# Attention kernel: sums of a row's halves and high parts of the values on ScalarE, grouped-query outputs read by ScalarE and added by GpSimd

## The chip, the cores and the metric

The kernel runs on one core of a Trainium2 chip. The metric is the device time of one execution in microseconds (us). Engines are named as the profile names them: PE is TensorE, DVE is VectorE, ACT is ScalarE, POOL is GpSimd, and SP is the engine whose queue issues the DMA transfers. Each engine carries out its own instructions in the order in which they stand in its queue; between engines, an instruction waits on semaphores for what it needs.

## What is computed

One layer of a hybrid block over 2048 latent tokens and 256 context tokens of width 1024: a modulated RMS norm, one input projection, three mixers (pooling, differential attention, grouped-query attention), a gate on each, and two output projections. The change touches the two attentions, which read 2304 keys (context and latent):

```python
def _diff_core(q, k, v, lam):              # 4 heads, two score maps each
    s = jnp.einsum('bqhcd,bkhcd->bhcqk', q, k).astype(jnp.float32) * (DIFF_HEAD_DIM ** -0.5)
    p = jax.nn.softmax(s, axis=-1)
    a = (p[:, :, 0] - lam * p[:, :, 1]).astype(v.dtype)
    return jnp.einsum('bhqk,bkhe->bqhe', a, v)

def _gqa_core(q, k, v):                    # 8 query heads, 2 key/value heads
    s = jnp.einsum('bqgrd,bkgd->bgrqk', q, k).astype(jnp.float32) * (GQA_HEAD_DIM ** -0.5)
    p = jax.nn.softmax(s, axis=-1).astype(v.dtype)
    return jnp.einsum('bgrqk,bkgd->bqgrd', p, v)
```

All values are 32-bit floats. The kernel feeds TensorE with 16-bit pairs, a high part and the remainder as a low part, and adds up the products.

## The kernel before

There are three stages. The first projects queries, keys and values and writes them to memory; it lasts until about 560 us. The second, from 560 to about 2330 us, is the attention, mixed with the gate projection (line 179), which is independent of it and fills PE. The third (from about 2404 us) is the branch and output projections. The change lies in the second stage alone.

**Rows.** The second stage goes through 256 *rows*. A row is 128 queries of one head against all 2304 keys. The rows come in fours: d0 and d1 (the two score maps of a differential head), then g0 and g1 (two query tiles of a grouped-query head). `score_row` does one row:

- PE writes the scores into two PSUM tiles, `sa` (1024 keys) and `sb` (1280 keys), of which there is one buffer each (L812).
- DVE takes the negated maximum of each half (L815, L816) and combines the two (L817), all into the small tile `nm` of four columns.
- ACT does the exponentials of both halves (L820, L821) into `pt`, each with the sum of its half accumulated into `nm` (columns 2 and 3). Only when these are done may PE write the next row's `sa` and `sb`.

**What follows a row.** `inverse_sum` on DVE adds the two half sums and scales them (L825), and takes the reciprocal (L827). For the differential rows it runs at the head of the next row's place; at d1 it is followed by the ratio of the two maps (L866). For grouped-query rows it stands at the head of the place two rows later, inside `high`. `combine` (DVE, L870) merges d0 and d1. `high` (ACT, L874 or L898) writes the 16-bit high part of the probabilities, `low` (DVE, L879 or L903) the remainder; both are transposed by DMA (L849), and the products with the values (`diff_av` L917, `gqa_av` L941 and L947) are done on PE four rows later.

**The order** of all engines is written out by hand: the order in which the Python code emits instructions is the order in each engine's queue. The loop over `i` emits, for each row: what tables `ahead` and `split_later` hold for this place, then the row, then `todo` and `after`, then PE's filling (products with the values, then gate units). On DVE a *slot*, from one L817 to the next, therefore reads: L817 of this row; splits of values, if any; `combine` or `low`; readings of PE's filling; then the small instructions at the head of the next place; the next row's L815 and L816. On ACT it reads: both exponentials; readings of PE's filling; `high` of an earlier row; the next exponentials.

**Readings of PE's filling.** A finished gate unit is read by ACT (`gt`, L188); in 48 units, those of the SiLU paths, DVE multiplies it (L191). A finished grouped-query product has its two halves in partitions 0 to 63 and 64 to 127 of PSUM: ACT copies the upper one (`sh`, L954), and DVE scales the lower one and adds (L955), into `ot`.

**Values.** When a head begins, `load_values` fetches its values in six parts of three key tiles. DVE writes the high part (L798) and the low part (L800) of each into `vt`. Two parts are split in one slot, so each load takes three slots. A differential load has parts of 128x384, a grouped-query load parts of 128x192.

## Time and profile before

| | |
|---|---|
| median of 3 runs | 2884.64 us (2880.09 to 2886.94) |
| the profiled execution | 2881.96 us, of which its span is 2880.2 us |
| busy, share of the span | PE 95%, DVE 77%, ACT 56%, POOL 24% |
| mean granted TensorE clock | 0.987 of full speed |

The span runs from the first to the last instruction; 1.8 us lie outside it. Busy time of PE is modelled and includes the pipelined end of every product, so a stretch in which PE is busy throughout is one without gaps, not one at the peak. The share of an engine over the whole span mixes stages with different limits; the second stage is read slot by slot below.

### The profile page before, as it was taken

The page shows a single profiled execution, that of the slowest core. Times are in us where ns is not written, and L with a number is a line of the kernel's source. Part 1 is how long each engine was busy: PE and PEld are TensorE (multiplying, and loading weights), DVE is VectorE, ACT ScalarE, POOL GpSimd, SP SyncE. Part 2 cuts the span into 40 slices and gives each one's busy share as a digit, 9 for nine tenths or more (in the row PEclk, how much of TensorE's full clock was granted, in tenths as well). Part 3 has the DMA queues.
Part 4 walks back from the last instruction along what each step waited for, and adds up shares of the span by engine and source line. Part 5 has one row for each costly group of instructions (what it writes and reads, how often), then busy time and mean ns, then how long its engine had stood idle before and what let it go on. Part 6 is the DMA issues. An engine that isn't in the chain of part 4 may idle for free. (4 is left out here: it accounts for less than half of the span.)

```text
span 2880.2 us, 41085 instructions
## 1 busy us (share of the span) xinstructions
PE 2739.0 (95%) x15031; PEld 1592.2 (55%) x15031; DVE 2216.1 (77%) x2829; ACT 1624.4 (56%) x2168; POOL 700.0 (24%) x699
## 2 busy tenths in 40 slices
PE   7999999999999989999989999999999988999999
PEld 2544435645555445545545555555555546787787
DVE  4446657499888898889989999899998956766753
ACT  3844432267766666767756777676777742322221
POOL 1035645411111102110202111112111114443421
PEclk8999999999999999999999999999999998999999
DMA  7345552488988888888898999998998876767664
GB/s 258 110 122 160 132 161 64 112 172 175 187 166 170 179 184 168 171 178 179 170 196 190 185 188 185 177 206 178 186 187 173 177 164 230 248 225 258 208 244 147
DMA packets 1134266, 516.46 MB, mean 179 GB/s; under 512 B 985040, under 2 KB 1038704, under 8 KB 1134064
## 3 DMA queue, kind: packets, MB, share of 16 engines
q1 hardware_dynamic: 1134064, 513.84, 75.9%
q8 instruction: 118, 1.93, 0.3%
q14 instruction: 84, 0.69, 0.1%
HBM read 208.24 MB, written 78.97 MB: 100 GB/s over the span
## 5 line engine op out<-in xcount | busy, mean ns | idle before, releaser
L179 PE MATMUL gate<-hT,gws 128*128 128x512 f16 x3840 | 871.6, 380 | 0.5 <-ACT gt L185 0.5
L179 PEld LDWEIGHTS <-gws 128*128 128x128 f16 x3840 | 368.6, 98 | 432.0 <-issue 32.9
L820 ACT ACTIVATE pt<-sa,nm,escale 128x1024 f32<-128x1024 f32 x256 | 308.4, 1205 | 427.0 <-DVE nm L817 387.6
L812 PEld LDWEIGHTS <-qt 128*128 128x128 f16 x2560 | 249.8, 98 | 380.5 <-issue 100.9
L532 PE MATMUL qkv<-wt,hT 128*128 128x512 f16 (+1 forms) x1920 | 391.6, 358 | 0.0
L816 DVE TENSOR_REDUCE nm<-sb 128x1 f32<-128x1280 f32 x256 | 378.9, 1480 | 2.1 <-PE sb L812 2.1
L821 ACT ACTIVATE pt<-sb,nm,escale 128x1280 f32<-128x1280 f32 x256 | 360.5, 1408 | 0.0
L815 DVE TENSOR_REDUCE nm<-sa 128x1 f32<-128x1024 f32 x256 | 310.8, 1214 | 49.6 <-PE sa L812 41.1
L903 DVE SCALAR_TENSOR_TENSOR lo<-pt,nm,hi 128x2304 f16<-128x2304 f32 x128 | 337.8, 2639 | 8.6 <-ACT hi L898 4.7
L812 PE MATMUL sb<-kt,qt 128*128 128x512 f16 (+1 forms) x1536 | 320.5, 345 | 24.9 <-ACT pt L821 24.7
L898 ACT ACTIVATE hi<-pt,nm 128x2304 f16<-128x2304 f32 x128 | 283.3, 2213 | 92.0 <-issue 46.7
L812 PE MATMUL sa<-kt,qt 128*128 128x512 f16 x1024 | 262.6, 379 | 35.9 <-ACT pt L820 35.0
L532 PEld LDWEIGHTS <-hT 128*128 128x128 f16 x1920 | 187.1, 98 | 173.7 <-issue 9.1
L1193 PE MATMUL br<-bt,wt 128*128 128x512 f32 x1152 | 268.6, 394 | 1.6 <-DVE wt L1048 1.6
L1193 PEld LDWEIGHTS br<-bt,wt 128*128 128x128 f32 x1152 | 217.9, 189 | 51.0 <-DVE wt L1048 2.7
L927 POOL TENSOR_TENSOR o<-ot 128x256 f32<-128x256 f32 x32 | 19.8, 620 | 837.3 <-ACT ot L923 706.9
L163 POOL TENSOR_SCALAR gws<-gw 128x512 f16<-128x512 f32 x74 | 69.3, 936 | 605.9 <-PE gate L179 602.2
L917 PE MATMUL av<-th,vt 128*128 128x256 f16 x1728 | 198.9, 273 | 0.0
L1225 PE MATMUL out<-y,wt 128*128 128x512 f32 x768 | 186.2, 401 | 11.6 <-DVE wt L1048 4.9
L917 PEld LDWEIGHTS <-vt 128*128 128x128 f16 x1728 | 169.1, 98 | 19.8
L1225 PEld LDWEIGHTS out<-y,wt 128*128 128x128 f32 x768 | 145.4, 190 | 51.5 <-DVE wt L1048 8.1
L870 DVE SCALAR_TENSOR_TENSOR pt<-pt,nm 128x2304 f32<-128x2304 f32 x64 | 168.9, 2640 | 0.0
(209 smaller groups left out, 3222.9 us busy)
## 6 DMA issues: line engine op xcount, KB each, us to landing
tD<-gt SPq DMA_DIRECT2D x96, 256.0 KB
wr<-in_w_br SPq DMA_DIRECT2D x32, 768.0 KB
ld<-tD SPq DMA_DIRECT2D x96, 256.0 KB
scan<-in_w_gate SPq DMA_DIRECT2D x40, 512.0 KB
gw<-in_w_gate SPq DMA_DIRECT2D x80, 256.0 KB
qt<-qD SPq DMA_DIRECT2D x256, 64.0 KB
wr<-in_w_out SPq DMA_DIRECT2D x32, 512.0 KB
sgD<-gt SPq DMA_DIRECT2D x48, 256.0 KB
```

The costliest lines, as they stand in the source:

```text
L179: nc.tensor.matmul(ps, lhsT=w[:, b, k, :], rhs=hT[k][:, a, c * CH:(c + 1) * CH], start=(n == 0), stop=(n == 3 * KT - 1))
L532: nc.tensor.matmul(ps[:, :width], lhsT=tokens_of(t, k, a), rhs=wt[k][:, b, :width], start=(n == 0), stop=(n == 3 * KT - 1))
L812: nc.tensor.matmul(dst, lhsT=qt[:, s, o * P:(o + 1) * P], rhs=kt[:, k0:k1], start=(s == 0), stop=(s == 1))
L815: nc.vector.tensor_reduce(out=nm[:, 0:1], in_=sa, axis=AX.X, op=ALU.max, negate=True)
L816: nc.vector.tensor_reduce(out=nm[:, 1:2], in_=sb, axis=AX.X, op=ALU.max, negate=True)
L820: nc.scalar.activation(out=pt[:, :SA], in_=sa, func=AF.Exp, scale=escale[:, m:m + 1], bias=nm[:, 0:1], accum_out=nm[:, 2:3])
L821: nc.scalar.activation(out=pt[:, SA:], in_=sb, func=AF.Exp, scale=escale[:, m:m + 1], bias=nm[:, 0:1], accum_out=nm[:, 3:4])
L898: nc.scalar.activation(out=box["hi"], in_=pt, func=AF.Copy, scale=nm[:, 3:4])
L903: nc.vector.scalar_tensor_tensor(out=lo, in0=pt, scalar=nm[:, 3:4], in1=box["hi"], op0=ALU.mult, op1=ALU.subtract)
L917: nc.tensor.matmul(ps[:, :256], lhsT=vt[:, k, v, :], rhs=pts[a][:, k, :], start=(n == 0), stop=(n == 3 * NKT - 1))
L1193: nc.tensor.matmul(ps, lhsT=wb[:, a, 4 * br + k, :], rhs=branch_tile(c, br, k)[:, b], start=(m == 0), stop=(m == 11))
L1225: nc.tensor.matmul(ps, lhsT=wo[:, a, k, :], rhs=ys[c, k // 2][:, k % 2, b, :], start=(m == 0), stop=(m == 3 * KT - 1))
```

## The change

Four edits, all in the second stage:

1. In `score_row`, two ACT instructions of one column follow the exponentials of each of the 256 rows: the sum of the second half is scaled, and the sum of the first half is scaled and added to it (L823 and L824 of the changed kernel). The DVE instruction L825 goes; `inverse_sum` is the reciprocal alone.
2. For grouped-query rows the reciprocal moves from inside `high`, two places later, to the head of the next place, where the differential rows have it already.
3. In `load_values`, the high part of the values is written by ACT; DVE still writes the low part, which reads the high one.
4. In `gqa_av`, ACT reads both halves of the product from PSUM, and GpSimd adds them in SBUF. `sh` is now a 128-partition tile, of which the matching 64 partitions are used.

```diff
             def split():
-                nc.vector.tensor_scalar(out=vt[:, :, 0, :], in0=vr, scalar1=vscale[:, m:m + 1], scalar2=None,
-                                        op0=ALU.mult)
+                nc.scalar.activation(out=vt[:, :, 0, :], in_=vr, func=AF.Copy, scale=vscale[:, m:m + 1])
                 nc.vector.scalar_tensor_tensor(out=vt[:, :, 1, :], in0=vr, scalar=vscale[:, m:m + 1],
                                                in1=vt[:, :, 0, :], op0=ALU.mult, op1=ALU.subtract)
...
             nc.scalar.activation(out=pt[:, SA:], in_=sb, func=AF.Exp, scale=escale[:, m:m + 1], bias=nm[:, 0:1], accum_out=nm[:, 3:4])
+
+            scale = 1.0 / PSC if m else lscale[:, 0:1]
+            nc.scalar.activation(out=nm[:, 3:4], in_=nm[:, 3:4], func=AF.Copy, scale=scale)
+            nc.scalar.activation(out=nm[:, 2:3], in_=nm[:, 2:3], func=AF.Identity, scale=scale, bias=nm[:, 3:4])
             return pt, nm
 
-        def inverse_sum(nm, scale):
-            nc.vector.tensor_scalar(out=nm[:, 2:3], in0=nm[:, 2:3], scalar1=nm[:, 3:4], scalar2=scale, op0=ALU.add,
-                                    op1=ALU.mult)
+        def inverse_sum(nm):
             nc.vector.reciprocal(out=nm[:, 3:4], in_=nm[:, 2:3])
...
             def high():
-                inverse_sum(nm, 1.0 / PSC)
                 box["hi"] = part("hi")
...
+            at(ahead, i + 1, lambda: inverse_sum(nm))
             at(ahead, i + 2, high)
             at(after, i + 2, low)
...
-            sh = sp.tile([64, 256], F32, name="sh", tag="o2", bufs=2)
+            sh = sp.tile([P, 256], F32, name="sh", tag="o2", bufs=2)[r0:r0 + 64]
             nc.scalar.activation(out=sh, in_=ps[64:128, :256], func=AF.Copy, scale=oscale[64:128, 1:2])
-            nc.vector.scalar_tensor_tensor(out=ot[r0:r0 + 64, :], in0=ps[0:64, :256], scalar=oscale[0:64, 1:2], in1=sh,
-                                           op0=ALU.mult, op1=ALU.add)
+            nc.scalar.activation(out=ot[r0:r0 + 64, :], in_=ps[0:64, :256], func=AF.Copy, scale=oscale[0:64, 1:2])
+            nc.gpsimd.tensor_tensor(out=ot[r0:r0 + 64, :], in0=ot[r0:r0 + 64, :], in1=sh, op=ALU.add)
```

**Where it moves instructions: two ordinary slots on DVE.** DVE's queue before, in the slots of a g0 and of a g1 row in the middle of the second stage (line numbers are those of each kernel; in the changed one L814, L815 and L816 are the maxima, L828 is the reciprocal; what a row waits for by semaphore stands in brackets):

```order
L817 TENSOR_SCALAR nm<-nm,escale 128x1 [waits DVE_49]
L870 SCALAR_TENSOR_TENSOR pt<-pt,nm 128x2304
L815 TENSOR_REDUCE nm<-sa 128x1 [waits PE_49]
L816 TENSOR_REDUCE nm<-sb 128x1 [waits PE_49]
L817 TENSOR_SCALAR nm<-nm,escale 128x1 [waits DVE_49]
L879 SCALAR_TENSOR_TENSOR lo<-pt,nm,hi 128x2304 [waits DMAHW1_49,Activation_49]
L955 SCALAR_TENSOR_TENSOR ot<-av,oscale,sh 64x256 [waits DMAHW4_49,Activation_49]
L825 TENSOR_SCALAR nm<-nm 128x1
L827 RECIPROCAL nm<-nm 128x1 [waits DVE_49]
L815 TENSOR_REDUCE nm<-sa 128x1 [waits PE_49]
```

The same two slots of DVE in the changed kernel:

```order
L816 TENSOR_SCALAR nm<-nm,escale 128x1 [waits DVE_49]
L871 SCALAR_TENSOR_TENSOR pt<-pt,nm 128x2304
L828 RECIPROCAL nm<-nm 128x1 [waits Activation_49]
L814 TENSOR_REDUCE nm<-sa 128x1 [waits PE_49]
L815 TENSOR_REDUCE nm<-sb 128x1 [waits PE_49]
L816 TENSOR_SCALAR nm<-nm,escale 128x1 [waits DVE_49]
L880 SCALAR_TENSOR_TENSOR lo<-pt,nm,hi 128x2304 [waits DMAHW1_49,Activation_49]
L828 RECIPROCAL nm<-nm 128x1 [waits Activation_49]
L814 TENSOR_REDUCE nm<-sa 128x1 [waits PE_49]
```

L955 and L825 are gone, and every slot now has one reciprocal ahead of the next maximum, which waits for ACT; the g0 slot had nothing there, and in the g1 slot L825 belonged to an earlier row and waited for nothing.

**The same g1 slot on ACT.** Before:

```order
L820 ACTIVATE pt,nm<-sa,nm,escale 128x1024 [waits DVE_49,PE_49,Activation_49]
L821 ACTIVATE pt,nm<-sb,nm,escale 128x1280 [waits PE_49]
L954 ACTIVATE sh<-av,oscale 64x256 [waits PE_49]
L898 ACTIVATE hi<-pt,nm 128x2304 [waits DMAHW3_49,DVE_49,Activation_49]
L820 ACTIVATE pt,nm<-sa,nm,escale 128x1024 [waits DVE_49,PE_49]
```

ACT in the changed kernel:

```order
L819 ACTIVATE pt,nm<-sa,nm,escale 128x1024 [waits DVE_49,PE_49]
L820 ACTIVATE pt,nm<-sb,nm,escale 128x1280 [waits PE_49]
L823 ACTIVATE nm<-nm 128x1 [waits Activation_49]
L824 ACTIVATE nm<-nm 128x1 [waits Activation_49]
L955 ACTIVATE sh<-av,oscale 64x256 [waits PE_49,Pool_49]
L956 ACTIVATE ot<-av,oscale 64x256 [waits DMAHW4_49]
L898 ACTIVATE hi<-pt,nm 128x2304 [waits DMAHW3_49]
```

The two sums stand directly behind the exponentials, each waiting for ACT's own result before it, and ahead of all readings of PE's filling.

**A slot in which values are split, on DVE.** Before (a d1 slot of the load of the second differential head):

```order
L817 TENSOR_SCALAR nm<-nm,escale 128x1 [waits DVE_49]
L798 TENSOR_SCALAR vt<-vr,vscale 128x3x128 [waits DMAHW2_49]
L800 SCALAR_TENSOR_TENSOR vt<-vr,vscale,vt 128x3x128 [waits DVE_49]
L798 TENSOR_SCALAR vt<-vr,vscale 128x3x128 [waits DMAHW3_49]
L800 SCALAR_TENSOR_TENSOR vt<-vr,vscale,vt 128x3x128 [waits DVE_49]
L903 SCALAR_TENSOR_TENSOR lo<-pt,nm,hi 128x2304 [waits DMAHW5_49,Activation_49]
L825 TENSOR_SCALAR nm<-nm,lscale 128x1 [waits Activation_49]
```

DVE in the changed kernel:

```order
L816 TENSOR_SCALAR nm<-nm,escale 128x1 [waits DVE_49]
L799 SCALAR_TENSOR_TENSOR vt<-vr,vscale,vt 128x3x128 [waits DMAHW2_49,Activation_49]
L799 SCALAR_TENSOR_TENSOR vt<-vr,vscale,vt 128x3x128 [waits DMAHW3_49,Activation_49]
L903 SCALAR_TENSOR_TENSOR lo<-pt,nm,hi 128x2304 [waits DMAHW5_49]
L828 RECIPROCAL nm<-nm 128x1
```

And ACT in that slot of the changed kernel:

```order
L819 ACTIVATE pt,nm<-sa,nm,escale 128x1024 [waits DVE_49,PE_49]
L820 ACTIVATE pt,nm<-sb,nm,escale 128x1280 [waits PE_49]
L823 ACTIVATE nm<-nm,lscale 128x1 [waits Activation_49]
L824 ACTIVATE nm<-nm,lscale 128x1 [waits Activation_49]
L798 ACTIVATE vt<-vr,vscale 128x3x128 [waits DMAHW2_49]
L798 ACTIVATE vt<-vr,vscale 128x3x128 [waits DMAHW3_49]
```

The high parts stand on ACT behind this row's exponentials and sums; the low parts on DVE, which stand ahead of `low`, wait for them.

## Rows read from the trace of the kernel before

**Rows 1.** The page, part 1: busy time, share and instructions of each engine.

```profile
PE 2739.0 (95%) x15031; PEld 1592.2 (55%) x15031; DVE 2216.1 (77%) x2829; ACT 1624.4 (56%) x2168; POOL 700.0 (24%) x699
```

**Rows 2.** Stretches: length, busy PE, PEld, DVE, ACT, POOL; clock; DMA share, GB/s.

```profile
701.66:1305.73 604.07, 563.75 (x3331) 303.43 (x3330) 533.09 (x608) 409.01 (x490) 90.90 (x82) 1.00 0.86 176
1163.22:1219.49 56.27, 52.90 (x316) 28.72 (x315) 49.73 (x56) 38.61 (x46) 6.09 (x7) 1.00 0.85 166
1605.39:1657.60 52.21, 52.21 (x321) 29.01 (x319) 47.23 (x52) 38.97 (x47) 7.80 (x7) 1.00 0.92 186
```

**Rows 3.** Timeline of DVE, a d1 slot: start, length (us), instruction, [idle before].

```profile
1200.14 0.27 DVE L817 TENSOR_SCALAR nm<-nm,escale 128x1 f32<-128x1 f32 x1
...
1203.24 0.27 DVE L825 TENSOR_SCALAR nm<-nm,lscale 128x1 f32<-128x1 f32 x1 [0.30 <-ACT pt L821]
1203.55 0.16 DVE L827 RECIPROCAL nm<-nm 128x1 f32<-128x1 f32 x1
...
1203.93 1.22 DVE L815 TENSOR_REDUCE nm<-sa 128x1 f32<-128x1024 f32 x1
...
1206.58 0.27 DVE L817 TENSOR_SCALAR nm<-nm,escale 128x1 f32<-128x1 f32 x1
```

**Rows 4.** Timeline of DVE, the g1 slot that follows after one more row.

```profile
1212.52 0.27 DVE L817 TENSOR_SCALAR nm<-nm,escale 128x1 f32<-128x1 f32 x1
...
1216.14 0.48 DVE L955 SCALAR_TENSOR_TENSOR ot<-av,oscale,sh 64x256 f32<-64x256 f32 x1 [0.82 <-ACT sh L954]
...
1216.77 0.16 DVE L827 RECIPROCAL nm<-nm 128x1 f32<-128x1 f32 x1
1216.85 1.21 DVE L815 TENSOR_REDUCE nm<-sa 128x1 f32<-128x1024 f32 x1
```

**Rows 5.** Timeline of DVE and ACT, a d1 slot with a SiLU gate unit.

```profile
1227.35 0.27 DVE L817 TENSOR_SCALAR nm<-nm,escale 128x1 f32<-128x1 f32 x1
...
1230.31 0.68 ACT L188 ACTIVATE gt<-gate,ginv 128x512 f32<-128x512 f32 x1
...
1231.02 0.69 DVE L191 SCALAR_TENSOR_TENSOR gt<-gt,gate 128x512 f32<-128x512 f32 x1 [0.88 <-ACT gt L188]
...
1231.63 0.27 DVE L825 TENSOR_SCALAR nm<-nm,lscale 128x1 f32<-128x1 f32 x1
```

**Rows 6.** Timeline of DVE, a d1 slot in which values are split.

```profile
1054.02 0.27 DVE L817 TENSOR_SCALAR nm<-nm,escale 128x1 f32<-128x1 f32 x1
...
1056.02 0.62 DVE L800 SCALAR_TENSOR_TENSOR vt<-vr,vscale,vt 128x384 f16<-128x384 f32 x1
1056.56 2.61 DVE L903 SCALAR_TENSOR_TENSOR lo<-pt,nm,hi 128x2304 f16<-128x2304 f32 x1
...
1062.43 0.27 DVE L817 TENSOR_SCALAR nm<-nm,escale 128x1 f32<-128x1 f32 x1
```

**Rows 7.** Groups by line, short ACT instructions: count | busy us, mean ns | idle before.

```profile
L613 ACT ACTIVATE ls<-ls 128x2 f32<-128x2 f32 x1 | 0.2, 204 | 9.2 <-DVE ls L612 9.2
L314 ACT ACTIVATE hC<-hf,hsd 128x256 f16<-128x256 f32 x4 | 2.0, 496 | 3.7 <-DVE hsd L133 3.7
L314 ACT ACTIVATE hT<-hf,hsd 128x128 f16<-128x128 f32 x4 | 1.5, 386 | 0.0
L300 ACT ACTIVATE hf<-tpx,shiftS,gainS 128x128 f32<-128x128 f32 x4 | 1.8, 457 | 0.0
```

**Rows 8.** Groups by line, DVE instructions that go, or wait for ACT.

```profile
L191 DVE SCALAR_TENSOR_TENSOR gt<-gt,gate 128x512 f32<-128x512 f32 x48 | 33.0, 687 | 40.2 <-ACT gt L188 40.2
L955 DVE SCALAR_TENSOR_TENSOR ot<-av,oscale,sh 64x256 f32<-64x256 f32 x64 | 30.5, 476 | 66.4 <-ACT sh L954 66.4
L798 DVE TENSOR_SCALAR vt<-vr,vscale 128x384 f16<-128x384 f32 x24 | 14.5, 604 | 0.0
```

**Rows 9.** Timeline of DVE and POOL, a stretch in which both read SBUF.

```profile
1235.16 2.83 DVE L870 SCALAR_TENSOR_TENSOR pt<-pt,nm 128x2304 f32<-128x2304 f32 x1
...
1235.55 4.57 POOL L165 TENSOR_TENSOR gws<-gw,gws 128x512 f16<-128x512 f32 x2
```

More of the change, by code (lines that the diff above doesn't have):

```diff
@@ L856, in diff_row @@
                 first[0] = pt, nm
-                at(ahead, i + 1, lambda: inverse_sum(nm, lscale[:, 0:1]))
+                at(ahead, i + 1, lambda: inverse_sum(nm))
                 return
@@ L863, in ratio @@
             def ratio():
-                inverse_sum(nm, lscale[:, 0:1])
+                inverse_sum(nm)
                 nc.vector.tensor_scalar(out=nm[:, 2:3], in0=nm[:, 3:4], scalar1=n0[:, 2:3], scalar2=neglam[:, 0:1],
@@ L905, in low @@
                 turn(lo, step, 1, o)
+            at(ahead, i + 1, lambda: inverse_sum(nm))
             at(ahead, i + 2, high)
```

## The prediction, made before the change was run

> **What bounds the kernel now.** The page first [rows 1]: PE is busy for 95% of the span, DVE for 77%. The share says little by itself, since only the second stage changes. So I read the second stage by stretches, cut at the L817 of a row, then two or three slots in the timeline.
>
> Stretches [rows 2]. In the later part of the stage (third line) eight slots take 52.21 us and PE is busy for all 52.21: there PE is the bound, at 26.1 us for four slots, and DVE, busy for 47.23, has 5 us to spare. In the part with the SiLU gate units (first line, 84 slots, 604.07 us; eight of them in the second line) eight slots take 56.27 us and PE is busy for 52.90: there something else sets the pace, by 4 us in eight slots. That stretch is what a relief of DVE could win: at PE's pace its 84 slots would take 84 x 6.53 = 548, 56 us less.
>
> What sets the pace is a loop through two engines. One d1 slot [rows 3]: from L817 to the next L817 are 6.44 us. DVE does `low` and is then idle for 0.30 us until ACT has finished both exponentials; 3.10 us after L817 the first small instruction can start. L825 and the reciprocal take 0.31 until L827, the ratio and the hand-over 0.38 more until L815; from L815 to L817 are 2.65. So in a differential slot DVE waits for ACT and ACT waits for DVE: 3.10 + 0.31 + 0.38 + 2.65 = 6.44. Anything put behind the exponentials on ACT, and waited for at the head of the next slot on DVE, lengthens this loop, however idle either engine is.
>
> In a g1 slot [rows 4] DVE also waits 0.82 us for `sh`, and L815 starts 4.33 us after L817. In a slot with a SiLU unit [rows 5] the unit's reading on ACT follows the exponentials, L191 waits 0.88 us for it, and the small instructions start only 4.28 us after L817 instead of 3.10.
>
> **The change part by part.**
>
> *Price of the sums on ACT.* No ACT instruction of one column on all partitions stands in the trace. The nearest are [rows 7]: two columns with constant scale 0.20 us; 128 columns with one scale from a tile 0.39, less 0.11 for 128 columns (0.50 - 0.39) gives 0.28; with scale and bias from tiles 0.46 - 0.11 = 0.35. A grouped-query row has a constant scale in the first sum and a bias from a tile in the second: 0.20 + 0.28 = about 0.5. A differential row has one and two tile operands: 0.28 + 0.35 = 0.63, and with the two hand-overs between dependent instructions about 0.7. Bounds: 0.4 (both at 0.20) and 0.9 (both at 0.46, no columns taken off).
> The Trainium skill, "ScalarE: Activation LUTs", What ACT_TABLE_LOAD costs, gives 186 ns with constants, 93 ns more for every operand from a tile: by that 0.47 and 0.65 before hand-overs, which would change the total by some 3 us. Its Rules for kernel authors put adding and multiplying on VectorE; here the trace shows that neither engine's price decides, but the place in the loop.
>
> *Ordinary slots.* Every slot now has one reciprocal at its head that waits for ACT's second sum, with L815 0.08 us behind it [rows 4], 0.38 at d1 [rows 3]. A slot of a grouped-query row: 3.10 + 0.5 + 0.08 + 2.65 = 6.33; d0: 6.53; d1: 6.83; four of them 26.0. In the PE-bound part that is as much as PE's 26.1. The two limits now touch, and a slot in which either is late is no longer made up in the next; I put 5 us on some 155 slots outside the SiLU part. The g1 slots lose the wait for `sh` and start L815 at 3.68 instead of 4.33; g0 slots, which waited for nothing (5.94 us from the last L817 of [rows 3] to the first of [rows 4]), grow by 0.4, d1 by 0.4. In the 35 ordinary slots of the SiLU part (15 g1, 11 d1, 7 g0, 2 d0) that is 15 x -0.65 + 11 x 0.4 + 7 x 0.4 + 2 x 0.4 = -2 us.
>
> *Slots with a SiLU unit,* 48 [rows 8]. `gt` on ACT now stands behind the sums, so L191 starts 0.5 or 0.7 later, and only the L825 behind it (0.31 with its hand-over) goes. d1: 0.7 - 0.31 = +0.4. d0 has two L825: +0.1. g0 has none and gets a reciprocal: 0.5 + 0.08 = +0.6. g1: 0.5 - 0.31, plus the second copy (about 0.4), which now also stands ahead of `gt`: +0.5 to +0.6. With 19, 9, 14 and 6 of them (d0, d1, g0, g1): 1.9 + 3.6 + 8.4 + 3.3 = +17 us.
>
> *Values.* L798 goes from DVE, 24 wide ones of 0.60 us [rows 8] and 12 narrow ones: 18 slots. But now both low parts, and `low` behind them, wait until ACT is through with this row's exponentials and sums and has written the high parts; before, all this ran beside the exponentials. A d1 slot: 3.10 + 0.7 + first high part (0.39 + 2 x 0.11 = 0.60) + two low parts (0.62 each [rows 6], the second high part ready in time) = 5.6; `low` 2.5; reciprocal, ratio 0.38; 2.65: 11.1 us, against 8.41 now [rows 6]. That is +2.7 for each of 12 slots, 32 us. In the six narrow slots the high part takes 0.28 + 0.16 and the low parts about 0.4 each, which gives 10 us for a slot; two of them are late for DMA already, the others gain 2 to 3: +10 us in all. Some of the first load's slots are long now for other reasons, so I take 40 us for all 18. Bounds: 20, if ACT's high parts come in time for half of them, and 50. DVE is simply idle for some 3.5 us in these slots; queued behind the waiting L799 are `low`, the reciprocal and both maxima, and PE waits for these through the exponentials.
>
> *Grouped-query outputs.* 64 DVE readings of 0.48 us and their 66 us of waiting go [rows 8]; the gain is in the g1 figures above, and in the PE-bound part it is worth nothing. ACT gets a second copy of 64x256, about 0.4 us paced. ACT as such has room: 38.97 of 52.21 us [rows 2] + 8 x 0.6 + 2 x 0.4 = 44.6. The GpSimd addition (1.0 us is POOL's mean instruction, 700.0 / 699 [rows 1]) delays only the store to memory, read in the third stage. Its bound is a contention: [rows 9] show `combine` at 2.83 us beside GpSimd's subtractions, against 2.61 for an operation of the same width [rows 6], so 64 x 0.22 = 14 us if every addition hit one. I take 0: the copies end some 0.8 us behind the sums, when DVE is at the maxima, which read PSUM.
> The Trainium skill, "GPSIMD Engine Reference", Specifications, says that GpSimd shares its SBUF access with VectorE and collides with VectorE instructions with two SBUF inputs; the rows agree (0.22 us), and by it alone the sum would be up to 14 us more.
>
> *Sum.* 5 - 2 + 17 + 40 = +60 us on the profiled execution's 2881.96 us (2880.2 of span and 1.8 around it): 2942. The median of the runs is 2.7 us above that execution, so **2945 us**, 2.1% slower.
>
> **The rivals.**
>
> *The relief wins (faster).* If the reciprocal did not have to wait for the sums, DVE's freed time would count where DVE's loop is the bound: 0.3 for L825 in 84 slots (25 us), 0.82 + 0.4 in 21 g1 slots (26 us), and two L798 in 18 slots (19 us), 70 us: 2815 us. For it: DVE is the busiest engine there, 49.73 of 56.27 [rows 2]. Against it: DVE already reaches the head of a d1 slot 0.30 us before ACT [rows 3], so ACT would have to be quicker than today, with two instructions more. It decides from the point where both sums take less than the 0.31 of L825; even 0.4 is above that. A half of it, say 2850, would need DVE's waits to be hidden by PE in the SiLU part too. 0.11 for both.
>
> *No change.* The sums at 0.4, and the wait for the high parts half hidden: SiLU slots +17 - 48 x 0.2 = +7, ordinary ones -9, values +20: +18 us, still above 0.2% (6 us). Within 0.2% needs a gain that I don't see: 0.05.
>
> *The stores block the transfers (much slower).* The store of `ot` now waits for GpSimd in SP's queue, and behind it stand the transposes of `hi` and `lo`, which PE needs four rows later. GpSimd may be at the split of gate weights (4.57 us for two subtractions [rows 9]) when the addition comes. If half of 64 additions come late by 4 us and PE waits for half of that, it is 32 x 2 = 64 us more: 3009 us. For it: the DMA share is 0.92 in the PE-bound part [rows 2]. Against it: the addition comes early in a slot, and in DVE's place the store already waited for `sh` [rows 4]. 0.10, together with sums at their upper bound (0.3 us on 250 slots, 75 us: 3020).
>
> **How the numbers follow.** Forecast 0.74, faster 0.11, same 0.05, much slower 0.10. The forecast's own range goes from 2910 (sums 0.4: about -25 us; values 20 to 30) to 2985 (sums 0.8, values 50, contention 14). The range that is asked for leaves out the faster case and the far end of the slower one: 2905 to 3005. A measurement of this kernel tells about 0.2% from no change. Faster 0.11, within 0.2% 0.05, slower 0.84.
>
> **What would show it.** Right: on DVE, each reciprocal idle for 0.5 to 1 us for ACT's L824 (some 200 in all); eight slots of the SiLU part at 57 to 58 us; the PE-bound part still near 52.2 to 53 for eight, now with small gaps on PE; slots with values at 10 to 11 us, L799 waiting over 3 us for L798 on ACT. DVE's busy share falls, ACT's rises by 200 us, and the time rises all the same. Wrong: reciprocals that start without a wait; SiLU stretches shorter than 56.27; L799 that follows L816 at once; or, on the other side, PE waiting for `th` in ordinary slots.

## The result, and the profile after

The changed kernel takes **2952.5 us** (median of four runs, 2950.9 to 2955.7), the kernel before 2883.5 beside it: a ratio of **1.0241**, 95% interval 1.0226 to 1.0256. It is 2.4% slower; 2945 us was forecast, in a range of 2905 to 3005. The profiled execution has a span of 2953.9 us, 73.7 more than before.

The page's busy line, beside [rows 1]: DVE falls from 77 to 71% of the span, ACT rises by 185 us, and the time rises all the same.

```profile
PE 2766.4 (94%) x15031; PEld 1599.1 (54%) x15031; DVE 2109.0 (71%) x2473; ACT 1809.4 (61%) x2780; POOL 754.4 (26%) x763
```

The three stretches of [rows 2], cut at the same rows' combining instruction (now L816); length, then busy PE, PEld, DVE, ACT, POOL, the clock, and what DMA did:

```profile
721.59:1350.68 629.09, 569.84 (x3330) 304.50 (x3329) 503.16 (x497) 466.33 (x686) 108.12 (x104) 0.99 0.83 169
1204.70:1263.02 58.32, 53.36 (x319) 28.86 (x318) 47.30 (x47) 43.70 (x65) 9.83 (x10) 1.00 0.81 159
1664.34:1717.29 52.95, 52.40 (x320) 29.08 (x320) 44.81 (x43) 43.88 (x65) 9.03 (x9) 1.00 0.89 183
```

The SiLU part grows from 604.07 to 629.09 us, its eight slots from 56.27 to 58.32. In the later part PE was busy for all of 52.21; now eight slots take 52.95 and PE has 0.55 us of gaps.

The waits (engine, line, tile, what it waited for: us in total, times, longest) show where DVE waits now:

```profile
DVE nm L828 <- ACT nm L824: 166.9, 190, 3.7
DVE gt L191 <- ACT gt L188: 73.3, 45, 2.7
DVE vt L799 <- ACT vt L798: 70.9, 18, 4.1
```

The first did not exist: 190 of the 256 reciprocals wait for ACT's second sum, 0.88 us each on the mean; all but two of the others stand behind an L191 or L799 that has waited for ACT already. L191 waited for 40.2 us before [rows 8] and waits for 73.3 now; L799 waits for L798 in all 18 slots, 3.9 us on the mean. Prices of the new instructions (count | busy us, mean ns):

```profile
L823 ACT ACTIVATE nm<-nm 128x1 f32<-128x1 f32 x128 | 26.0, 203 | 4.0
L824 ACT ACTIVATE nm<-nm 128x1 f32<-128x1 f32 x128 | 37.7, 295 | 4.2
L824 ACT ACTIVATE nm<-nm,lscale 128x1 f32<-128x1 f32 x128 | 49.5, 387 | 4.3
L957 POOL TENSOR_TENSOR ot<-ot,sh 64x256 f32<-64x256 f32 x64 | 48.0, 749 | 788.7 <-ACT ot L956 618.4 <-issue 151.4 <-DMA uD<-gt 18.7
```

One g1 slot in the timeline (start, length, instruction, [idle before]), the counterpart of [rows 4]:

```profile
1256.64 0.27 DVE L816 TENSOR_SCALAR nm<-nm,escale 128x1 f32<-128x1 f32 x1
...
1257.01 1.20 ACT L819 ACTIVATE pt<-sa,nm,escale 128x1024 f32<-128x1024 f32 x1 [0.66 <-DVE nm L816]
...
1259.51 0.19 ACT L820 ACTIVATION_READ_ACCUMULATOR pt<-sb,nm,escale 128x1 f32 x1
1259.73 0.20 ACT L823 ACTIVATE nm<-nm 128x1 f32<-128x1 f32 x1
1259.97 0.29 ACT L824 ACTIVATE nm<-nm 128x1 f32<-128x1 f32 x1
1260.29 0.47 ACT L955 ACTIVATE sh<-av,oscale 64x256 f32<-64x256 f32 x1
1260.30 0.16 DVE L828 RECIPROCAL nm<-nm 128x1 f32<-128x1 f32 x1 [0.86 <-ACT nm L824]
...
1260.79 0.47 ACT L956 ACTIVATE ot<-av,oscale 64x256 f32<-64x256 f32 x1
1261.16 2.20 ACT L898 ACTIVATE hi<-pt,nm 128x2304 f16<-128x2304 f32 x1
...
1263.02 0.27 DVE L816 TENSOR_SCALAR nm<-nm,escale 128x1 f32<-128x1 f32 x1
1263.39 1.20 ACT L819 ACTIVATE pt<-sa,nm,escale 128x1024 f32<-128x1024 f32 x1
```

The loop is there as described: L816, exponentials, sums, reciprocal, maxima, L816, 6.38 us. But ACT is also busy without a break from 1257.01 to the next exponential, which is 6.38 us too. Over the span ACT is at 61%; in this slot it is full. Here two limits stand at the same 6.38 us, the loop and ACT's own work.

A d1 slot with values, the counterpart of [rows 6], 10.97 us instead of 8.41:

```profile
1087.55 0.27 DVE L816 TENSOR_SCALAR nm<-nm,escale 128x1 f32<-128x1 f32 x1
...
1090.97 0.39 ACT L824 ACTIVATE nm<-nm,lscale 128x1 f32<-128x1 f32 x1
1091.26 1.11 ACT L798 ACTIVATE vt<-vr,vscale 128x384 f16<-128x384 f32 x2
1091.89 1.15 DVE L799 SCALAR_TENSOR_TENSOR vt<-vr,vscale,vt 128x384 f16<-128x384 f32 x2 [4.07 <-ACT vt L798]
1092.96 2.61 DVE L903 SCALAR_TENSOR_TENSOR lo<-pt,nm,hi 128x2304 f16<-128x2304 f32 x1
...
1098.52 0.27 DVE L816 TENSOR_SCALAR nm<-nm,escale 128x1 f32<-128x1 f32 x1
```

The TensorE clock is not what makes the slots with values long. The second stage has a mean granted clock of 0.99 now and had 1.00 before; two g0 slots with values, from 623.01 and from 2013.35 us, had 0.84 and 0.67 and take 10.47 us each.

All 255 slots, summed by kind from the timelines of DVE (us), forecast beside measured. Two of the 48 SiLU slots also split values and stand with the values:

| slots | before | after | measured | forecast |
|---|---|---|---|---|
| ordinary, outside the SiLU part (156) | 1035.8 | 1050.0 | +14.2 | +5 |
| ordinary, in the SiLU part (35) | 230.4 | 229.5 | -0.9 | -2 |
| with a SiLU unit (46) | 347.9 | 366.3 | +18.4 | +17 |
| with values (18) | 150.7 | 187.6 | +36.9 | +40 |
| all | 1764.8 | 1833.4 | +68.6 | +60 |

The other 5 us of the span lie outside these slots: the first slot starts 3.8 us later, and 1.4 us come behind the last. In the profiles of the kernels below the first slot starts anywhere from 561.5 to 569.9 us, though none changes the first stage; 563.2 before and 566.9 after lie within that, so I count the 3.8 as scatter.

### The profile page after: what moved, and what is told of

The parts are those of the page before. It is cut to its first block, busy times and chain, and to the rows that moved or that the text cites. A ratio compares the mean times of both kernels' runs of the same rounds, so it can differ in the third digit from the quotient of the medians.

```text
span 2953.9 us, 41343 instructions
## 1 busy us (share of the span) xinstructions
PE 2766.4 (94%) x15031; PEld 1599.1 (54%) x15031; DVE 2109.0 (71%) x2473; ACT 1809.4 (61%) x2780; POOL 754.4 (26%) x763
## 3 DMA queue, kind: packets, MB, share of 16 engines
q1 hardware_dynamic: 1134064, 513.84, 73.7%
## 4 chain that ended last, share of the span: by engine, by line
PE 34%; ACT 27%; DVE 25%; DMA 6%; issue 4%; SPq 2%; POOL 1%; ACTq 0%; DVEq 0%; POOLq 0%
ACT pt L820 9%; ACT pt L819 9%; PE qkv L532 8%; DVE nm L815 8%; PE br L1194 8%; DVE nm L814 7%; PE out L1226 6%; PE gate L179 5%; ACT hi L898 2%; ACT nm L823 2%; DVE nm L816 2%; PE sb L811 2%; DMA th<-lo 2%; ACT nm L824 1%; PE sa L811 1%
## 5 line engine op out<-in xcount | busy, mean ns | idle before, releaser
L819 ACT ACTIVATE pt<-sa,nm,escale 128x1024 f32<-128x1024 f32 x256 | 307.7, 1202 | 376.0 <-DVE nm L816 366.4
L815 DVE TENSOR_REDUCE nm<-sb 128x1 f32<-128x1280 f32 x256 | 379.1, 1481 | 1.0 <-PE sb L811 1.0
L811 PE MATMUL sb<-kt,qt 128*128 128x512 f16 (+1 forms) x1536 | 329.2, 351 | 28.1 <-ACT pt L820 26.6
L903 DVE SCALAR_TENSOR_TENSOR lo<-pt,nm,hi 128x2304 f16<-128x2304 f32 x128 | 337.3, 2635 | 24.7 <-ACT hi L898 14.4
L814 DVE TENSOR_REDUCE nm<-sa 128x1 f32<-128x1024 f32 x256 | 309.5, 1209 | 24.4 <-PE sa L811 23.4
L532 PEld LDWEIGHTS <-hT 128*128 128x128 f16 x1920 | 189.6, 99 | 176.9 <-issue 11.1
L957 POOL TENSOR_TENSOR ot<-ot,sh 64x256 f32<-64x256 f32 x64 | 48.0, 749 | 788.7 <-ACT ot L956 618.4
L871 DVE SCALAR_TENSOR_TENSOR pt<-pt,nm 128x2304 f32<-128x2304 f32 x64 | 168.6, 2635 | 0.0
L880 DVE SCALAR_TENSOR_TENSOR lo<-pt,nm,hi 128x2304 f16<-128x2304 f32 x64 | 167.5, 2616 | 1.5 <-ACT hi L875 0.7
```

What stands on the lines that cost most here:

```text
L532: nc.tensor.matmul(ps[:, :width], lhsT=tokens_of(t, k, a), rhs=wt[k][:, b, :width], start=(n == 0), stop=(n == 3 * KT - 1))
L811: nc.tensor.matmul(dst, lhsT=qt[:, s, o * P:(o + 1) * P], rhs=kt[:, k0:k1], start=(s == 0), stop=(s == 1))
L814: nc.vector.tensor_reduce(out=nm[:, 0:1], in_=sa, axis=AX.X, op=ALU.max, negate=True)
L815: nc.vector.tensor_reduce(out=nm[:, 1:2], in_=sb, axis=AX.X, op=ALU.max, negate=True)
L819: nc.scalar.activation(out=pt[:, :SA], in_=sa, func=AF.Exp, scale=escale[:, m:m + 1], bias=nm[:, 0:1], accum_out=nm[:, 2:3])
L903: nc.vector.scalar_tensor_tensor(out=lo, in0=pt, scalar=nm[:, 3:4], in1=box["hi"], op0=ALU.mult, op1=ALU.subtract)
```

## The experiments

The theory: the time is lost where work stands on the loop between ACT and DVE, whatever the engines' busy shares. The main rival: ACT's added busy time, or the transfers behind the new stores.

**One edit undone, or one alone.** First, the values' high parts back on DVE, the rest as changed:

```diff
-                nc.scalar.activation(out=vt[:, :, 0, :], in_=vr, func=AF.Copy, scale=vscale[:, m:m + 1])
+                nc.vector.tensor_scalar(out=vt[:, :, 0, :], in0=vr, scalar1=vscale[:, m:m + 1], scalar2=None,
+                                        op0=ALU.mult)
```

> The changed kernel with the values' high parts back on VectorE. Theory (low parts queue behind ScalarE's exponentials and sums): the 18 slots with values fall from 10.4 us on the mean to about 8.2, in all 37 to 40 us less than the changed kernel: 2912 to 2916 us, ratio to before 1.010 to 1.012. Rival (the loss of the changed kernel comes from GpSimd's additions and the stores behind them): these slots get shorter, but the total stays within 10 us of the changed kernel's 2952.

Measured: 2913.1 us, ratio 1.0103 (1.0088 to 1.0118). Second, the sums back on DVE (`inverse_sum` and its places as before), values and outputs as changed:

```diff
-            nc.scalar.activation(out=nm[:, 3:4], in_=nm[:, 3:4], func=AF.Copy, scale=scale)
-            nc.scalar.activation(out=nm[:, 2:3], in_=nm[:, 2:3], func=AF.Identity, scale=scale, bias=nm[:, 3:4])
...
-        def inverse_sum(nm):
+        def inverse_sum(nm, scale):
+            nc.vector.tensor_scalar(out=nm[:, 2:3], in0=nm[:, 2:3], scalar1=nm[:, 3:4], scalar2=scale, op0=ALU.add,
+                                    op1=ALU.mult)
```

> The changed kernel with the sums of the halves back on VectorE, and the reciprocal of the grouped-query rows two places later again, as before; values and outputs stay changed. Theory (the sums lengthen the loop between VectorE and ScalarE): the SiLU slots fall back (18 us), the ordinary slots outside the SiLU part return to TensorE's pace, 6.53 us (14 us), the ordinary ones of the SiLU part lose the wait for sh and gain nothing (12 us under before); the slots with values stay at 10 to 10.6 us: about 2900 to 2910 us, ratio 1.006 to 1.010. Rival (ScalarE's or GpSimd's mere load): no less than 2935.

Measured: 2903.6 us, 1.0068 (1.0053 to 1.0083). Third and fourth, the kernel before with the outputs' edit alone (the `gqa_av` part of the diff), and with the sums' edits alone:

> The kernel before with only the grouped-query outputs changed (read by ScalarE, added by GpSimd). Theory: VectorE no longer waits for sh; this is worth something only in the SiLU part, where VectorE's loop sets the pace (15 ordinary g1 slots of 7.02 us, down to 6.3 or less), and nothing where TensorE does: 10 to 15 us less than before, 2868 to 2873, ratio 0.995 to 0.997. Rival (stores wait for GpSimd and hold up the transposes, or contention): above before, 1.002 or more.

> The kernel before with only the sums on ScalarE and the reciprocal of each row at the head of the next place; values and outputs as before. Theory: ordinary slots 6.56 (d0), 6.88 (d1), 6.38 (g0) as in the changed kernel, but g1 slots now have the wait for sh behind the sums as well, 7.15 us; slots with values no longer than before: about 58 us more than before, 2935 to 2945, ratio 1.018 to 1.021. Rival (the sums cost only where the values do): ratio below 1.008.

Measured: outputs alone 2870.3 us, **0.9956** (0.9941 to 0.9971), the one edit that gains; sums alone 2941.1 us, 1.0200 (1.0183 to 1.0217). All four came out as expected. The slots of each (us):

| kernel | values, 18 | SiLU, 46 | first rows and SiLU part, ordinary, 49 | later part, ordinary, 142 | all |
|---|---|---|---|---|---|
| before | 150.7 | 347.9 | 321.8 | 944.4 | 1764.8 |
| outputs alone | 151.0 | 350.6 | 310.9 | 942.1 | 1754.6 |
| outputs and values | 180.4 | 350.3 | 311.6 | 938.8 | 1781.1 |
| sums alone | 148.1 | 363.8 | 338.5 | 975.8 | 1826.3 |
| outputs and sums | 148.0 | 366.4 | 324.6 | 952.9 | 1791.9 |
| all (after) | 187.6 | 366.3 | 324.3 | 955.2 | 1833.4 |

The price of the values stands in the values' slots: with the sums on ACT, undoing the values' edit takes 39.6 us from these slots and 1.9 from all others. Without the sums the same edit costs these slots 29.4 us; with them the high parts stand behind two more instructions. Of the SiLU slots' 18 us the sums alone bring 16; the outputs' edit adds 2.6 to 2.7, with or without the sums. The edits don't add up: the outputs' edit is worth 12 us without the sums and 28 us with them (2941.1 to 2913.1), because in a g1 slot the wait for `sh` came behind the sums as well, and with the sums it is no longer hidden by PE in the later part (975.8 to 952.9).

In the later part the outputs' edit alone takes away all of DVE's wait for `sh` and gains 2 us in 142 slots. One g1 slot there, DVE in the kernel with outputs alone:

```profile
1624.59 0.21 DVE L825 TENSOR_SCALAR nm<-nm 128x1 f32<-128x1 f32 x1
1624.83 0.16 DVE L827 RECIPROCAL nm<-nm 128x1 f32<-128x1 f32 x1
1625.63 1.23 DVE L815 TENSOR_REDUCE nm<-sa 128x1 f32<-128x1024 f32 x1 [0.64 <-PE sa L812]
```

DVE comes to the maximum early and waits for PE instead: in the kernel before DVE waited 0.82 us for `sh` in this slot, as in [rows 4]; now it waits for the scores.

**The sums' place.** Is it their place in the loop, or that ACT has them to do? First, the reciprocal of a grouped-query row back two places later, in `high`; the sums stay on ACT:

```diff
             def high():
+                inverse_sum(nm)
                 box["hi"] = part("hi")
...
-            at(ahead, i + 1, lambda: inverse_sum(nm))
```

> The changed kernel with one thing undone: the reciprocal of a grouped-query row stands again where it is needed, two rows later, so it no longer waits for ScalarE's sums at the head of the next row; the sums themselves stay on ScalarE, and differential rows are as changed. If the price of the sums is the wait at the head of the next slot (my theory), the slots behind a grouped-query row lose that wait: about 0.5 us in the 14 + 6 with a SiLU unit is kept by the SiLU reading, the ordinary ones fall back to the pace of TensorE. 2920 to 2932 us, ratio 1.013 to 1.017. If the time is lost because ScalarE has two more instructions to run, whoever waits for them (rival), nothing changes: 2948 to 2956 us, ratio 1.023 to 1.025.

Measured: 2947.0 us, 1.0217 (1.0193 to 1.0240): far above my range, just under the rival's. The runs lie between 2941.3 and 2954.9 us, so the 5.5 us to the changed kernel are within their scatter. The profiled execution, one of the fast ones (2942.6), lost 10.6 us in the slots, not 20 to 30. The wait did go, by half, but much of it became a wait for PE (8 times, 23.4 us in the changed kernel):

```profile
DVE nm L828 <- ACT nm L824: 80.9, 89, 3.7
DVE nm L814 <- PE sa L811: 66.5, 90, 7.6
```

The ordinary g0 slots of the later part fell from 6.38 to 5.97 us on the mean, so there the place was the price. But the d0 slots rose from 6.75 to 6.87 and g1 from 6.76 to 6.85, since PE needs its 26.1 us for four slots however they are divided. In the SiLU part most ordinary g1 slots fell from 6.38 to 5.92, and here the rival was half right: ACT needs as long as before from these exponentials to the next ones, so the next ones start late. One such slot and the start of the d0 slot behind it:

```profile
858.58 0.27 DVE L816 TENSOR_SCALAR nm<-nm,escale 128x1 f32<-128x1 f32 x1
858.95 1.20 ACT L819 ACTIVATE pt<-sa,nm,escale 128x1024 f32<-128x1024 f32 x1 [1.55 <-DVE nm L816]
...
864.50 0.28 DVE L816 TENSOR_SCALAR nm<-nm,escale 128x1 f32<-128x1 f32 x1
865.34 1.19 ACT L819 ACTIVATE pt<-sa,nm,escale 128x1024 f32<-128x1024 f32 x1
```

DVE's slot takes 5.92 us, ACT's round 6.39. So the 18 d0 slots with a SiLU unit rose from 7.88 to 8.17: by 0.06 for the reciprocal of g1 that now stands in each, and by 0.3 to 0.5 more in the 11 that follow a g1 slot of 5.92. My expectation had taken the gain of each slot by itself.

Next, one more copy of one column on ACT, put between the exponentials and the sums:

```diff
+            nc.scalar.activation(out=nm[:, 2:3], in_=nm[:, 2:3], func=AF.Copy, scale=1.0)
             nc.scalar.activation(out=nm[:, 3:4], in_=nm[:, 3:4], func=AF.Copy, scale=scale)
```

> The changed kernel with the suspected cost raised: one more ScalarE copy of one column, in place on the second exponential's sum, ahead of the two sums in every row (the value is unchanged). It takes 0.20 us, and the following sum needs its result. If work behind the exponentials lies on the loop of the two engines (my theory), each of some 250 slots grows by 0.20 to 0.23 us: 48 to 58 us more than the changed kernel, 3000 to 3012 us, ratio 1.040 to 1.045. If ScalarE, busy for 61% of the span, has room for it (rival), the time stays at 2950 to 2956 us.

Measured: 2954.0 us, 1.0239 (1.0223 to 1.0254), as the rival had it. The timeline of ACT tells why it decides nothing:

```profile
1253.56 0.20 ACT L820 ACTIVATION_READ_ACCUMULATOR pt<-sb,nm,escale 128x1 f32 x1
1253.65 0.19 ACT L823 ACTIVATE nm<-nm 128x1 f32<-128x1 f32 x1
1253.79 0.20 ACT L824 ACTIVATE nm<-nm 128x1 f32<-128x1 f32 x1
1254.02 0.29 ACT L825 ACTIVATE nm<-nm 128x1 f32<-128x1 f32 x1
```

The copy takes the first half's sum (not the second's, as the expectation has it), which is long ready, so it starts 0.09 us after the reading of the accumulator began. The sum behind it needs that reading and could start only 0.22 us after it in the changed kernel (1259.51, 1259.73); here 0.23. The copy ran in a gap in which ACT had been waiting for itself. I had put it where the loop has a hole. So the test was made again from both sides: the copy where nothing hides it, and the first sum where the gap hides it.

```diff
             nc.scalar.activation(out=nm[:, 2:3], in_=nm[:, 2:3], func=AF.Identity, scale=scale, bias=nm[:, 3:4])
+            nc.scalar.activation(out=nm[:, 2:3], in_=nm[:, 2:3], func=AF.Copy, scale=1.0)
```

> The changed kernel with one more ScalarE copy of one column behind the two sums, in place on their result, so that it starts only when the second sum is through and the reciprocal waits for it (the value is unchanged). 0.20 us and 0.04 of hand-over. By the loop theory each of some 255 slots grows by 0.24 us, since none has slack left: 55 to 61 us more than the changed kernel, 3003 to 3014 us, ratio 1.041 to 1.045. If the earlier extra copy was free because ScalarE has room for it anyhow (rival), this one is free too: 2948 to 2958 us.

```diff
-            nc.scalar.activation(out=nm[:, 3:4], in_=nm[:, 3:4], func=AF.Copy, scale=scale)
-            nc.scalar.activation(out=nm[:, 2:3], in_=nm[:, 2:3], func=AF.Identity, scale=scale, bias=nm[:, 3:4])
+            nc.scalar.activation(out=nm[:, 2:3], in_=nm[:, 2:3], func=AF.Copy, scale=scale)
+            nc.scalar.activation(out=nm[:, 2:3], in_=nm[:, 3:4], func=AF.Identity, scale=scale, bias=nm[:, 2:3])
```

> The changed kernel with the two sums in the other order: the first instruction scales the first exponential's sum, which is ready early, the second scales the second's and adds the first. ScalarE runs the same two instructions with the same durations; only the first no longer waits for the second exponential's accumulator, and should run in the 0.1 us or so in which ScalarE waits for it now. If the place of the sums on the loop through the two engines is what costs (my theory), the second sum ends 0.13 us earlier in each slot that the loop sets: 15 us in the 113 slots of the SiLU part, the first rows and the values, and up to 19 in the 142 others if TensorE lets them: 2918 to 2938 us, ratio 1.012 to 1.019. If it is the time for which ScalarE is busy (rival), nothing changes: 2948 to 2956 us.

Measured: the dependent copy 3009.2 us, 1.0431 (1.0415 to 1.0447), 56.8 us over the changed kernel, and the slots 53.2 more. The same two sums in the other order 2930.6 us, 1.0162 (1.0147 to 1.0177), 21.9 us less, with 25.7 us fewer in the slots. Both are inside the theory's ranges and outside the rival's. The clean tests are the g0 and d1 slots, in which ACT waits for L816 before its exponentials and so has room: in the later part their medians go from 6.38 and 6.88 us to 6.61 and 7.12 with the copy, and to 6.23 and 6.74 in the other order. A g1 slot of the first, then the same slot of the second:

```profile
1283.42 0.20 ACT L825 ACTIVATE nm<-nm 128x1 f32<-128x1 f32 x1
...
1283.66 0.17 DVE L829 RECIPROCAL nm<-nm 128x1 f32<-128x1 f32 x1 [1.10 <-ACT nm L825]
```

```profile
1246.81 0.19 ACT L820 ACTIVATION_READ_ACCUMULATOR pt<-sb,nm,escale 128x1 f32 x1
1246.90 0.19 ACT L823 ACTIVATE nm<-nm 128x1 f32<-128x1 f32 x1
1247.13 0.29 ACT L824 ACTIVATE nm<-nm 128x1 f32<-128x1 f32 x1
...
1247.45 0.17 DVE L828 RECIPROCAL nm<-nm 128x1 f32<-128x1 f32 x1 [0.72 <-ACT nm L824]
```

The reciprocal waits 1.10 us in the first, 0.86 in the changed kernel, 0.72 in the second. A copy of 0.20 us costs nothing in one place and 57 us in another. The place decides; only in the g1 slots, where ACT is full as well, can the runs not tell the two apart.

**The values' place.** ACT's high parts (now `f`) ahead of the row's exponentials instead of behind them; the low parts (`g`) stay:

```diff
-            split_later.append(load_values(key, src, c0, n, m, p))
+            f, g = load_values(key, src, c0, n, m, p)
+            at(ahead, row_now[0] + 1, f)
+            split_later.append(g)
```

> The changed kernel with one thing moved: ScalarE writes the high parts of the values ahead of the row's exponentials instead of behind them; all other instructions are the same. If the 37 us of the slots with values are the wait for the exponentials (my theory), these 18 slots fall from about 10.4 to 7 us, below the 8.4 of the kernel before: 60 us less than the changed kernel, 2885 to 2900 us, ratio 1.001 to 1.006. If the values' DMA or the slower copy on ScalarE is what costs (rival), the wait only moves to the exponentials, which now stand behind a copy that waits for the transfer: 2940 to 2960 us.

Measured: 2903.8 us, 1.0065 (1.0050 to 1.0080), 49 us less than the changed kernel; a little above the range. The slots with values fall from 187.6 to 136.8 us, 7.6 each, less than the 8.4 of before, and the others stay within 0.3 us in sum: the 37 us were the wait for the exponentials, not the price of the copy. In the two longest of them, 9.8 and 10.4 us, ACT waits 5.0 and 3.3 us for the values' transfer. The stage's granted clock is 1.00 here, and the slots without values are no shorter for it. With the sums on DVE again, which keeps of the change only what the runs speak for:

> A kernel that keeps of the change what the runs so far speak for: outputs as changed, sums on VectorE as before, and the values' high parts on ScalarE but ahead of the row's exponentials. The outputs' edit alone gave 2870; the slots with values should fall from 8.4 to about 7.1 us, since only the two low parts are left on VectorE: 18 x 1.3 = 23 us. 2842 to 2856 us, ratio 0.985 to 0.990. If ScalarE waits for the values' transfer ahead of the exponentials in more of these slots than the four of the run with early values, the gain is gone: 2865 to 2880 us.

Measured: 2861.7 us, **0.9924** (0.9908 to 0.9941), faster than both kernels, but between the expected range and the rival's. The slots with values take 138.9 us, 7.7 each; 12.9 us of it is DVE waiting for L798, 10.4 in three of them. In one of the three:

```profile
1467.56 0.80 ACT L798 ACTIVATE vt<-vr,vscale 128x192 f16<-128x192 f32 x2 [3.81 <-DMA vr<-gvD]
...
1468.05 0.77 DVE L801 SCALAR_TENSOR_TENSOR vt<-vr,vscale,vt 128x192 f16<-128x192 f32 x2 [3.29 <-ACT vt L798]
1468.26 1.19 ACT L821 ACTIVATE pt<-sa,nm,escale 128x1024 f32<-128x1024 f32 x1
```

ACT itself waits for the transfer there, and the exponentials are queued behind. That is the expectation's own rival, in part.

**Values on GpSimd.** Neither ACT nor DVE does anything for values; with the outputs' edit, and without it:

```diff
+                nc.gpsimd.tensor_scalar(out=vr, in0=vr, scalar1=vscale[:, m:m + 1], scalar2=1.0, op0=ALU.mult,
+                                        op1=ALU.mult)
+                nc.gpsimd.tensor_scalar(out=vt[:, :, 0, :], in0=vr, scalar1=1.0, scalar2=1.0, op0=ALU.mult,
+                                        op1=ALU.mult)
+                nc.gpsimd.tensor_tensor(out=vt[:, :, 1, :], in0=vr, in1=vt[:, :, 0, :], op=ALU.subtract)
```

> The kernel before with the outputs' edit alone (second copy on ScalarE, addition on GpSimd) and the values split wholly on GpSimd (scaled in place, high part copied, low part subtracted), so that neither ScalarE nor VectorE has anything to do for values. If the slots with values are long only for what these engines do in them, all 18 fall from 8.4 us to the 6.4 of an ordinary slot: 36 us less than with the outputs' edit alone, 2832 to 2842 us, ratio 0.982 to 0.986. If GpSimd's three instructions on each half (perhaps 1.5 us each, beside VectorE's reads of SBUF) come too late for the transposes and products that need the values, or slow `low`, the gain is halved or gone: 2852 to 2875 us.

> The kernel before with the values split wholly on GpSimd and nothing else (outputs read and added as before). With both edits the slots with values fell by 27 us, but as much came back in slots that waited for transposes, behind stores that wait for GpSimd. If GpSimd's additions of the outputs are what is in the way there (the rival of the prediction, stores that block the transfers), the gain stays without them: 2848 to 2858 us, ratio 0.988 to 0.992. If shorter slots simply find the transposes late, whoever adds, the same amount comes back: 2875 to 2888 us, ratio 0.997 to 1.002.

Measured: 2871.1 us, 0.9949 (0.9932 to 0.9966), and 2877.3 us, 0.9978 (0.9969 to 0.9988). In both the slots with values fall by 27 us (150.7 to 124.2 and 124.0). In the first, the ordinary slots rise by 21 us against outputs alone; in the second, by 19 against before. So GpSimd's additions of the outputs, and the stores that wait for them (the prediction's rival), are not what takes the gain. The kernel with values alone shows one of the long g1 slots (11.40 us; it is itself one of the 18 that split values):

```profile
1486.66 2.98 PE L942 MATMUL av<-th,vt 128*128 128x256 f16 x18 [3.20 <-DMA th<-hi]
...
1491.55 0.47 ACT L955 ACTIVATE sh<-av,oscale 64x256 f32<-64x256 f32 x1 [3.39 <-PE av L948]
```

PE waits for a transpose. Five slots that took 6.5 to 7.9 us before take 9.4 to 15.3, 21 us more in all, and with the outputs' edit the same slots are long: in four of them PE waits for a transpose as here, in one DVE does. In the longest PE also waited for GpSimd's high part. Which transfer in the queue makes these transposes late, now that the rows come faster, was not tried.

## Why the prediction was right, and where it was off

*The loop* was the right reading. It forecast 6.33 us for grouped-query slots, 6.53 for d0 and 6.83 for d1 where the loop sets the pace. Measured, as medians of the later part: 6.38, 6.73 and 6.88; in the SiLU part d0 has 6.56. Undoing the sums alone gives back 49 us of the 69. Where only the loop sets the pace, a chain behind the exponentials that is 0.24 us longer or 0.14 shorter moves the slot by 0.23 and 0.15 us. The eight slots of the SiLU part were put at 57 to 58 us and take 58.3.

*The price of the sums* was taken at 0.5 and 0.7 us. From the reading of the accumulator to the reciprocal in the g1 slot the two sums add 0.24 + 0.33 = 0.57 us, of 203 and 295 ns of their own; in a differential row, with one and two operands from tiles, they take 294 and 387 ns, 0.72 us from the start of the first to the end of the second in the d1 slot above. By the Trainium skill, "ScalarE: Activation LUTs", What ACT_TABLE_LOAD costs, each operand from a tile adds 93 ns; the rows' steps are 92 and 92. The same section lets instructions that follow each other overlap by about 93 ns. The trace shows that for the first high part in the d1 slot, which needs nothing of the sum before it and starts 0.10 us before that sum ends. But the second sum, which needs the first, starts 0.04 us after its end, and so do `sh` and `ot` in the g1 slot (0.03), though they need nothing of the one before.

*The ordinary slots outside the SiLU part* are the term that was mis-sized: +5 forecast, +14.2 measured. Four slots of the loop were put at 26.0 us, just below PE's 26.1, so that PE would go on setting the pace. Where only the loop acts they take 6.56 + 6.88 + 6.38 + 6.38 = 26.2, above PE's: each slot was 0.03 to 0.05 too short. And d0 is longer than its loop in more than half of the later part. Of 36 d0 slots there, 15 take 6.56; in 13, of 6.73 to 7.05, L814 starts just behind PE's scores; in 8, of 6.99 to 7.13, the exponentials start 0.8 to 0.95 us after L816 instead of 0.37. One of these:

```profile
1375.72 2.21 ACT L898 ACTIVATE hi<-pt,nm 128x2304 f16<-128x2304 f32 x1
1376.88 0.27 DVE L816 TENSOR_SCALAR nm<-nm,escale 128x1 f32<-128x1 f32 x1
1377.83 1.19 ACT L819 ACTIVATE pt<-sa,nm,escale 128x1024 f32<-128x1024 f32 x1
```

ACT is still writing `hi` of an earlier row, behind the sums, `sh`, `ot` and the gate's reading of the g1 slot. I had given ACT's room as an average of eight slots (44.6 of 52.2 us); the full g1 slot above has none. In sum, the 31 fours of the later part without values and without a long wait go from 26.21 to 26.40 us on the mean, 6.0 of the later part's 10.8. Most of the rest, 4.5, lies in three fours that took 29 to 33 us before; these were not followed up. The other 3.4 us lie in the 14 slots of the first rows.

*The SiLU slots* came out kind by kind: d0 +0.13, d1 +0.43, g0 +0.60, g1 +0.73 us against +0.1, +0.4, +0.6 and +0.5 to 0.6. *The values* came out close: the d1 slot shown was put at 11.1 and takes 10.97, the narrow ones about 10 and 9.9. In sum the twelve wide slots grew by 26.6 us, not 32, and the six narrow ones by 10.3.

*The outputs* gained where they were said to, in the g1 slots of the SiLU part without a unit: 7.02 to 6.41 us each, against 0.65 forecast. GpSimd's addition (0.75 us) costs nothing that can be seen: L903 takes 2635 ns, 2639 before.

*The rivals.* The relief loses because 190 of the 256 reciprocals wait for ACT, and nearly all others stand behind an instruction that does; DVE's freed 107 us became waiting. The stores did not block: PE's waits for transposed parts rose only from 13.8 to 19.8 us in sum.

## What to carry to other kernels

Where two engines wait for each other in every step and nothing else sets the pace, an instruction on that loop costs its full time, on the idle engine as on the busy one, unless it falls into a gap of the loop; read the loop from the timeline before moving work to the engine with the lower share. A share over a stage hides single steps in which the idle engine is full. Moving work out of one slot's wait pays only until the next limit, here PE, ACT's own work and the transposes, so add up a whole period of slots, not each slot alone.

## What the runs showed of the hardware

A small ACT instruction that needs an accumulator's sum starts 0.22 us after the reading of that accumulator began; one that does not starts after 0.09. An independent instruction of 0.20 us fits between them for 0.01 us. Where two half sums are combined, scaling the one that is ready first costs 22 us less over 256 rows than scaling the last.

GpSimd's scaling of 128x384 values takes 0.58 us, and 2.89 where it begins beside DVE's `low`, which reads two tiles of SBUF (kernel with outputs and values on GpSimd):

```profile
1067.15 2.64 DVE L880 SCALAR_TENSOR_TENSOR lo<-pt,nm,hi 128x2304 f16<-128x2304 f32 x1
1067.36 2.89 POOL L798 TENSOR_SCALAR vr<-vr,vscale 128x384 f32<-128x384 f32 x1
```

The scaling ends 0.46 us after `low` does, as if it had waited for it. All seven 128x384 scalings of this kernel that begin 0.16 to 1.42 us into such a DVE instruction end 0.45 us after it and take 1.64 to 2.90 us. Where a GpSimd instruction of the split began first, it kept its 0.51 to 0.91 us and DVE's took up to 3.10. So the one that begins later waits for the other; that they share a way to SBUF is inferred from this, and no run was made on it.
